# Root and reciprocal of the variance per output tile, and new ties for the first tiles' work

## The chip, the cores and the metric

The kernel runs on one core of a Trainium2 chip. That core has a matrix engine (PE; its weight loads are shown as PEld), a vector engine (DVE), an activation engine (ACT), GpSimd (POOL), and a queue engine (SP) that issues nearly all transfers between the device memory and the on-chip memory. Each engine works through its own list of instructions in order; an instruction that waits holds up all that stands behind it on its engine. The metric is the device time of one execution in microseconds (us), as the median of several runs; lower is better.

## The reference, cut to what matters

The kernel computes one layer of an encoder for two requests of 512 and 1024 tokens (1536 in all, 1024 features), with 16 learned tokens put in front. The change touches the normalisation of the convolution branch:

```
z   = rms_norm(h) @ w_in              # gates, values, q, k, v
y   = depthwise_conv(val * sigmoid(glu)) + conv_b
mu  = mean(y)                         # over 1024 channels, per token
var = mean((y - mu)**2)
c   = silu((y - mu) * rsqrt(var + 1e-5) * ln_g + ln_b) * silu(c_gate)
a   = neighbourhood_attention(q, k, v) * silu(a_gate)
out = h + rms_norm([c ; a] @ w_out)
```

## The kernel before, in words

Three stages follow each other on PE. First the input projections and the convolution (the convolution's taps run on DVE). Then the attention: 8 pairs of heads, each with 3 groups of tokens in 2 halves. For each block PE makes scores (`ss`, L578), DVE and ACT make the softmax (`pt`, L585 to L591), PE transposes (`tp`, L600), ACT copies the transposed block (`pT`, L602), and PE weighs the values with it (`po`, L616). Between these blocks PE's list is filled with projections of 24 matrix products (`mm`, L180): the keys and queries of the next pair, and gates of the attention branch, whose results ACT copies out (`ag`, L342). The last six of these projections, for gates 6 and 7 in three groups, stand behind the last weighted values (`a_gate(6, 7)`, L706).

The last stage is the output product (`py`, L794), in 12 tiles t of 128 tokens. A tile has two parts of 8 feature blocks: part 0 is the convolution branch, part 1 the attention branch. `mix(t, part)` loads one part (`mx`) and its gate (`gt`), normalises (part 0 alone: L767 subtracts the mean, L768 multiplies by the reciprocal root, L770 is the Silu of 8 blocks), multiplies with the Silu of the gate (L771, L772), and splits the product in a high and a low half (`mh` on ACT, L773; `ml` on DVE for the tiles 0 and 1, else on POOL, L774). The buffers of part 0, `mx`, `gt` and `mb`, are single, and all tiles share them. The output weights are loaded in 16 blocks and split the same way (`load_wo`, L731 to L750: ACT casts, DVE subtracts); blocks 0 to 5, 8, 9, 12 and 13 come through two buffers `wraw` that the gates' weights use too, so that a load waits until an earlier block's split is done. For the tiles 0 and 1 the products are made together: part 0 of tile 0, part 0 of tile 1, then the parts 1 (L810 to L814).

Mean and variance of each token come from `statistics()` (L648), which runs in small steps between the attention's blocks. It stores both in a table `std` in device memory (L666). At its end it loads all variances as 128x12 (`rv`, L674), takes the root on ACT (L678) and the reciprocal on DVE (L679), and stores them back over the variances (L680), four bytes at each place. `moments(t)` (L752) loads the two rows of tile t, spread over the partitions, into `mb`.

The order on each engine is not the order of the program text: a scheduler with a model of the times lays the instructions out, engine by engine. `tc.issue_after(x)` puts each instruction of its block that runs on the engine of `x` behind `x` in that engine's list; it adds no wait by itself. Before the change part 0 of tile 0 is tied behind the last copy of a transposed block (`last_pt`, an ACT instruction, L776), and part 0 of tile 1 behind the copy of the last gate (`last_copy`, ACT, L782).

Of the kernel before, what the change touches and what calls it, by code (L numbers as in the profile page):

```python
# [10 lines left out]
F32 = mybir.dt.float32  # L11
F32R = mybir.dt.float32r
AF = mybir.ActivationFunctionType
ALU = mybir.AluOpType
# [6 lines left out]
TG = TP + TS  # L21
# [72 lines left out]
def tile_encoder(ctx: ExitStack, tc: tile.TileContext, mt, xn, w_main, w_v, wo, cw, cb, lg, lb, pg, postg, rbt, rmask, y):  # L94
    nc = tc.nc
# [3 lines left out]
    mad = [tc.dram_tile((DC, 128, 512), F32, name=f"mad{g}") for g in range(3)]  # L99
# [3 lines left out]
    std = tc.dram_tile((2, TG), F32, name="std")  # L103

    const = ctx.enter_context(tc.tile_pool(name="const", bufs=1))
# [10 lines left out]
    nc.vector.memset(eps_sb[:, 1:2], 1e-5)  # L116

    ident = const.tile([128, 128], F32, name="ident")
    rv = const.tile([128, TG // 128], F32, name="rv")
    sel = const.tile([128, 16], F32, name="sel")  # L120
    cw_sb = const.tile([128, DC, 32], F32, name="cw_sb")
    cb_sb = const.tile([128, DC], F32, name="cb_sb")
# [158 lines left out]
        nc.scalar.copy(out=zc.rearrange("p (b r c) -> p b r c", r=8, c=8), in_=z[:, i].rearrange("p (r b c) -> p b r c", r=8, b=8))  # L281
        nc.sync.dma_start(zs[i][c], zc)

    vws, metas, last_copy = {}, [], [None]

    def load_v(qv):
        raws, his, los = [], [], []
# [46 lines left out]
    def gates(base, dst, cs):  # L334

        ws = [use_w(base + c) for c in cs]
        for g in range(3):
            for c, (wh, wl) in zip(cs, ws):
                ps = new_mm()
                proj(ps, wh, wl, 16 + g * 512, 16 + g * 512 + 512)  # L340
                gt = gpool.tile([128, 512], F32, name="ag", tag="ag", bufs=2)
                last_copy[0] = nc.scalar.copy(out=gt, in_=ps).ins  # L342
                nc.sync.dma_start(dst[g][c], gt)
                yield

# [219 lines left out]
    def scores(p, g, hf):  # L565
        if hf == 0:
            load_values(p, g)
        kh, kl = kbufs[p]
        qh, ql = qbuf.pop((p, g, hf))
        R8 = GR[g]["R"] * 8  # L570
        for jj in range(4):
            j = hf * 4 + jj
            b0, nk, key, _, _, e = block(g, j)
            ra, rn, ro = GR[g][key]
            w = rn * 8
            ss = ps_s.tile([128, 512], F32, name="ss")
            for i, (q, k) in enumerate(((qh, kh), (qh, kl), (ql, kh))):
                last_qk[0] = nc.tensor.matmul(ss[:, :nk * w], lhsT=q[:, jj].rearrange("p h x -> p (h x)"),  # L578
                                 rhs=k[:, b0:b0 + nk, ra:ra + rn, :].rearrange("p b r c -> p b (r c)"),
                                 start=(i == 0), stop=(i == 2))  # L580
            sv_ = ss[:, :nk * w].rearrange("p (k x) -> p k x", k=nk)[:, :, ro * 8:ro * 8 + R8]
            pt = apool.tile([128, 312], F32, name="pt", bufs=PTB)
            pv = pt[:, :nk * R8]
            sm = apool.tile([128, 4], F32, name="sm", bufs=8)
            nc.vector.tensor_tensor_reduce(out=pv.rearrange("p (k x) -> p k x", k=nk), in0=sv_,  # L585
                                           in1=e.rearrange("p k r c -> p k (r c)"), scale=1.0,
                                           scalar=-3.0e38, op0=ALU.add, op1=ALU.max, accum_out=sm[:, 0:1])
            nc.vector.tensor_scalar(out=sm[:, 1:2], in0=sm[:, 0:1], scalar1=-1.0, scalar2=None, op0=ALU.mult)  # L588
            last[0] = nc.scalar.activation(out=pv, in_=pv, func=AF.Exp, bias=sm[:, 1:2], scale=1.0, accum_out=sm[:, 2:3])  # L589
            nc.vector.reciprocal(sm[:, 3:4], sm[:, 2:3])  # L590
            nc.vector.tensor_scalar(out=pv, in0=pv, scalar1=sm[:, 3:4], scalar2=None, op0=ALU.mult)  # L591
            pts[p, g, j] = pv

    def transposes(p, g, hf):
# [10 lines left out]
    def weighted(p, g, hf):  # L605
        if hf == 0:
            pos[p, g] = ps_o.tile([128, 8, 64], F32, name="po")
        po, vt = pos[p, g], vts[p, g]
        for j in range(hf * 4, hf * 4 + 4):
            b0, _, _, nt, kt, _ = block(g, j)  # L610
            pT = pTs.pop((p, g, j))
            for k in range(nt):
                for h in range(2):
                    hs = slice(h * 64, h * 64 + 64)
                    v = vt[:, k, b0, hs] if g == 0 else vt[:kt, b0 + k, hs]
                    last_pv[0] = nc.tensor.matmul(po[hs, j, :], lhsT=v, rhs=pT[:kt, k * 128 + h * 64:k * 128 + h * 64 + 64],  # L616
                                                  start=(k == 0), stop=(k == nt - 1)).ins
        if hf == 1:
            mo = apool.tile([128, 512], F32, name="mo", bufs=1)
            nc.vector.tensor_copy(out=mo, in_=pos.pop((p, g)).rearrange("p j x -> p (j x)"))  # L620
            nc.sync.dma_start(mad[g][p], mo)

    def inner_gates():
        for p in (3, 4, 5):
# [23 lines left out]
    def statistics():  # L648
        for t in range(TG // 128):
            tsl = slice(t * 128, t * 128 + 128)  # L650
            hx = []
            for k in range(2):
                x = gpool.tile([128, 512], F32, name="ag", tag="ag", bufs=2).rearrange("p (c t) -> p c t", c=8)
                a = t % 4 * 128 + k * 64
                nc.sync.dma_start(x, zs[t // 4][:, :, a:a + 64].rearrange("c p t -> p c t"))
                hx.append((x, slice(k * 64, k * 64 + 64)))
            yield
            for moment in range(2):
                for x, sl in hx:
                    nc.vector.tensor_reduce(out=ms[:, sl], in_=x.rearrange("p c t -> p t c"), op=ALU.add, axis=mybir.AxisListType.X)  # L660
                yield
                ps = new_mm()
                with tc.issue_after(last_mm[0]):
                    nc.tensor.matmul(ps[:, :128], lhsT=ones, rhs=ms, start=True, stop=True)
                nc.scalar.copy(out=row[0:1], in_=ps[0:1, :128])
                nc.sync.dma_start(std[moment:moment + 1, tsl], row[0:1])  # L666
                if moment == 0:
                    for x, sl in hx:
                        nc.vector.tensor_tensor(out=x, in0=x, in1=ps[:, sl].unsqueeze(1).broadcast_to([128, 8, 64]), op=ALU.subtract)
                        nc.scalar.activation(out=x, in_=x, func=AF.Square)  # L670

        s = std[1:2]
        var = bass.AP(s.tensor, s.offset, [[1, 128], [128, TG // 128]])
        nc.sync.dma_start(rv, var)  # L674
        yield
        yield
        with tc.issue_after(last[0].ins):
            nc.scalar.activation(out=rv, in_=rv, func=AF.Sqrt, bias=eps_sb[:, 1:2])  # L678
        nc.vector.reciprocal(rv, rv)  # L679
        nc.sync.dma_start(var, rv)  # L680
        yield

    stats = statistics()
    knext, last_pv, last_pt = [None], [None], [None]
    e_build(0)
    groups = [(p, g, hf) for p in range(NPAIR) for g in range(3) for hf in range(2)]
    for n in range(len(groups) + 2):
# [64 lines left out]
    def moments(t):  # L752
        tsl = slice(t * 128, t * 128 + 128)
        s = std[:, tsl]
        nc.sync.dma_start(mb, bass.AP(s.tensor, s.offset, [[0, 128], [TG, 2], [1, 128]]))

    def mix(t, parts=(0, 1)):
        for part in parts:
            if part == 0:
                moments(t)  # L760
            mx, gt = mxs[part], gts[part]
            mh, ml = [x[t % 2 * 2 + part] for x in (mhs, mls)]
            g, csl = t // 4, slice(t % 4 * 128, t % 4 * 128 + 128)
            nc.sync.dma_start(mx, (zs, mad)[part][g][:, :, csl].rearrange("c p t -> p c t"))
            nc.sync.dma_start(gt, (cgd, agd)[part][g][:, :, csl].rearrange("c p t -> p c t"))
            if part == 0:
                nc.vector.tensor_tensor(out=mx, in0=mx, in1=mb[:, 0:1].broadcast_to([128, 8, 128]), op=ALU.subtract)  # L767
                nc.vector.tensor_tensor(out=mx, in0=mx, in1=mb[:, 1:2].broadcast_to([128, 8, 128]), op=ALU.mult)  # L768
                for c in range(8):
                    nc.scalar.activation(out=mx[:, c], in_=mx[:, c], func=AF.Silu, scale=lg_sb[:, c:c + 1], bias=lb_sb[:, c:c + 1])  # L770
            nc.scalar.activation(out=gt, in_=gt, func=AF.Silu)  # L771
            nc.vector.tensor_tensor(out=mx, in0=mx, in1=gt, op=ALU.mult)  # L772
            nc.scalar.copy(out=mh, in_=mx)  # L773
            (nc.vector if t < MLT else nc.gpsimd).tensor_tensor(out=ml, in0=mx, in1=mh.bitcast(F32), op=ALU.subtract)  # L774

    with tc.issue_after(last_pt[0]):  # L776
        mix(0, (0,))
    for n in range(16):
        if n == 6:
            mix(0, (1,))  # L780
        elif n == 8:
            with tc.issue_after(last_copy[0]):  # L782
                mix(1, (0,))
        elif n == 10:
            mix(1, (1,))
        load_wo(n)
    pgb = wop.tile([128, D], F32, name="pgb")
# [124 lines left out]
```

## Time and profile before

| what | value |
|---|---|
| median of 3 runs | 1469.12 us (1467.73 to 1469.58) |
| the profiled execution | 1470.34 us |
| its span in the trace | 1468.2 us |
| mean granted clock of PE | 0.993 |
| PE busy | 1437.6 us (98%) |
| DVE, ACT, POOL busy | 1012.4, 562.8, 254.9 us |

The trace shows one execution. A row of the chain of waits gives a piece of the work that ended last: its start, its length, and the engine and line, or the transfer. A row of a timeline gives start and length of an instruction, and in brackets how long its engine stood idle before it and for what. A row of windows gives the busy time of each engine in a stretch, with the number of instructions in brackets, the granted clock of PE (1.00 is its upper level, 0.50 half of it), the share of the transfer engines that was busy, and GB/s.

### The profile page before, as it was taken

Reading aid. Unit: us, or ns where it says so; the run is one execution under the profiler, and the core shown is the slowest. Engines: PE = TensorE matmul, PEld = TensorE weight load, DVE = VectorE, ACT = ScalarE, POOL = GpSimd, SP = SyncE. Lnnn points to the kernel's source line nnn. Section 1 sums busy time; section 2 is a strip of 40 time slices with the busy share of each in tenths; the row PEclk is TensorE's granted clock in tenths of the full one; section 3 lists DMA queues with packets and bytes.
Section 4 is the critical chain, followed back from the end, with each engine's and each line's share of the span. In section 5 each row is a group of like instructions: output and inputs, shape, how many; then the busy total and the mean of one; then the engine's idle time right before and its main releaser. Section 6 shows DMA issues by size and latency. Waiting matters only on the chain.

```text
span 1468.2 us, 24129 instructions
## 1 busy us (share of the span) xinstructions
PE 1437.6 (98%) x9536; PEld 1239.6 (84%) x9536; DVE 1012.4 (69%) x1739; ACT 562.8 (38%) x1299; POOL 254.9 (17%) x188
## 2 busy tenths in 40 slices
PE   7999999999999999999999999999979989999998
PEld 6988998988998888888888988888868878888886
DVE  6599999998999899846776777767544364342431
ACT  7311112112111111235564555655534466544440
POOL 2042022112101211221111211111101002122120
PEclk9999999999999999999999999999989999999999
DMA  8113113312231212242232232332322495544521
GB/s 266 42 48 117 47 55 110 93 40 93 76 92 50 96 51 86 105 105 75 77 88 79 84 82 77 88 87 83 86 62 87 159 294 145 151 147 136 164 89 43
DMA packets 153464, 145.19 MB, mean 99 GB/s; under 512 B 37216, under 2 KB 125432, under 8 KB 153352
## 3 DMA queue, kind: packets, MB, share of 16 engines
q1 hardware_dynamic: 153352, 143.67, 32.5%
q8 instruction: 74, 1.21, 0.3%
q14 instruction: 38, 0.31, 0.1%
HBM read 105.35 MB, written 42.72 MB: 101 GB/s over the span
## 4 chain that ended last, share of the span: by engine, by line
PE 90%; DMA 4%; ACT 2%; DVE 2%; POOL 1%; issue 1%; DVEq 0%; SPq 0%; ACTq 0%; POOLq 0%
PE mm L180 36%; PE py L794 18%; PE tp L180 9%; PE mm L322 5%; PE ss L578 5%; PE po L180 5%; PE po L616 4%; PE tp L600 4%; PE tp L322 3%; DMA wraw<-in_wo 1%; PE po L322 1%; POOL vl L142 1%; DMA std<-rv 1%; DMA yo<-in_wo 0%; ACT mx L770 0%
## 5 line engine op out<-in xcount | busy, mean ns | idle before, releaser
L180 PE MATMUL mm<-uw,whi 128*128 128x512 f32 (+2 forms) x1904 | 562.1, 372 | 0.0
L272 DVE SCALAR_TENSOR_TENSOR z<-ub,cw_sb,z 128x1536 f32<-128x1536 f32 (+2 forms) x270 | 498.7, 1854 | 8.1
L180 PEld LDWEIGHTS mm<-uw,whi 128*128 128x128 f32 x1904 | 342.5, 188 | 55.4 <-issue 1.3
L180 PE MATMUL mm<-uw,wlo 128*128 128x512 f32 (+2 forms) x952 | 352.6, 371 | 1.1 <-POOL wlo L142 1.1
L142 POOL TENSOR_TENSOR wlo<-wraw,whi 128x1024 fp32r<-128x1024 f32 x48 | 129.0, 2689 | 542.2 <-ACT whi L141 537.5
L180 PEld LDWEIGHTS mm<-uw,wlo 128*128 128x128 f32 x952 | 179.4, 188 | 27.2 <-POOL wlo L142 1.4
L794 PE MATMUL py<-uw,mh 128*128 128x512 f32 x576 | 182.0, 397 | 0.0
L180 PE MATMUL tp<-uw,whi 128*128 128x512 f32 (+2 forms) x512 | 132.9, 344 | 0.0
L589 ACT ACTIVATE pt<-pt,sm 128x216 f32<-128x216 f32 (+4 forms) x192 | 97.2, 507 | 92.9 <-DVE sm L588 79.9
L794 PEld LDWEIGHTS py<-uw,mh 128*128 128x128 f32 x576 | 108.7, 189 | 25.9
L794 PE MATMUL py<-uw,ml 128*128 128x512 f32 x288 | 113.8, 395 | 0.0
L602 ACT COPY pT<-tp 108x256 f32<-108x256 f32 (+4 forms) x192 | 77.9, 419 | 81.9 <-PE tp L600 57.1
L180 PEld LDWEIGHTS tp<-uw,whi 128*128 128x128 f32 x512 | 89.3, 188 | 11.6
L767 DVE TENSOR_TENSOR mx<-mx,mb 128x1024 f32<-128x1024 f32 x12 | 14.7, 1225 | 121.2 <-DMA mx<-zs 110.0
L585 DVE CUSTOM_DVE_ANT_0 pt<-ss,ei 128x216 f32<-128x216 f32 (+2 forms) x144 | 62.6, 437 | 50.2 <-PE ss L578 26.6
L180 PE MATMUL tp<-uw,wlo 128*128 128x512 f32 (+2 forms) x256 | 88.1, 344 | 0.0
L600 PE MATMUL tp<-ident,pt 128*96 128x128 f32 (+2 forms) x480 | 85.5, 275 | 0.3 <-ACT pT L602 0.2
L774 POOL TENSOR_TENSOR ml<-mx,mh 128x1024 fp32r<-128x1024 f32 x20 | 48.2, 2430 | 211.5 <-ACT mh L773 193.7
L322 PE MATMUL mm<-vh,uw 128*128 128x256 f32 x448 | 83.5, 285 | 0.7 <-DVE uw L208 0.5
L591 DVE TENSOR_SCALAR pt<-pt,sm 128x216 f32<-128x216 f32 (+4 forms) x192 | 70.7, 368 | 4.9
L578 PE MATMUL ss<-kh,qh 128*128 128x264 f32 (+3 forms) x192 | 65.3, 340 | 9.0 <-DVE sm L585 9.0
L141 ACT CAST whi<-wraw 128x1024 fp32r<-128x1024 f32 x48 | 50.2, 1047 | 61.6 <-DMA wraw<-in_w_main 19.1
(170 smaller groups left out, 2183.1 us busy)
## 6 DMA issues: line engine op xcount, KB each, us to landing
wraw<-in_w_main SPq DMA_DIRECT2D x48, 512.0 KB
xt<-in_xn SPq DMA_DIRECT2D x12, 512.0 KB
vd<-vs SPq DMA_DIRECT2D x96, 64.0 KB
zs<-zc SPq DMA_DIRECT2D x24, 256.0 KB
cgd<-ag SPq DMA_DIRECT2D x24, 256.0 KB
agd<-ag SPq DMA_DIRECT2D x24, 256.0 KB
ag<-zs SPq DMA_DIRECT2D x24, 256.0 KB
mad<-mo SPq DMA_DIRECT2D x24, 256.0 KB
```

The source lines that it names most:

```text
L142: eng.tensor_tensor(out=lo, in0=raw, in1=hi.bitcast(F32), op=ALU.subtract)
L180: last_mm[0] = nc.tensor.matmul(ps[:, :n], lhsT=w[:, dc, :], rhs=u[dc // 4][:, dc % 4, :], start=(dc == 0 and i == 0), stop=(dc == DC - 1 ...
L272: nc.vector.scalar_tensor_tensor(out=zv, in0=ub[:, a:b, k:k + 512], scalar=cw_sb[:, c, k:k + 1], in1=zv, op0=ALU.mult, op1=ALU.add)
L322: nc.tensor.matmul(ps[:, :256], lhsT=u[dc // 4][:, dc % 4, :], rhs=w[dc // 4][:, dc % 4, :], start=(dc == 0 and i == 0), stop=(dc == DC - ...
L578: last_qk[0] = nc.tensor.matmul(ss[:, :nk * w], lhsT=q[:, jj].rearrange("p h x -> p (h x)"), rhs=k[:, b0:b0 + nk, ra:ra + rn, :].rearrange ...
L585: nc.vector.tensor_tensor_reduce(out=pv.rearrange("p (k x) -> p k x", k=nk), in0=sv_, in1=e.rearrange("p k r c -> p k (r c)"), scale=1.0, ...
L589: last[0] = nc.scalar.activation(out=pv, in_=pv, func=AF.Exp, bias=sm[:, 1:2], scale=1.0, accum_out=sm[:, 2:3])
L591: nc.vector.tensor_scalar(out=pv, in0=pv, scalar1=sm[:, 3:4], scalar2=None, op0=ALU.mult)
L600: nc.tensor.transpose(out=tp[:kt, k * 128:k * 128 + 128], in_=pv[:, k * kt:k * kt + kt], identity=ident)
L602: last_pt[0] = nc.scalar.copy(out=pT[:kt, :nt * 128], in_=tp[:kt, :nt * 128]).ins
L616: last_pv[0] = nc.tensor.matmul(po[hs, j, :], lhsT=v, rhs=pT[:kt, k * 128 + h * 64:k * 128 + h * 64 + 64], start=(k == 0), stop=(k == nt - ...
L794: nc.tensor.matmul(pss[hf], lhsT=m[e // 8][:, e % 8], rhs=w[e][:, hf * 512:hf * 512 + 512], start=(n == 0 and i == 0), stop=(n == 15 and i ...
```

## The change

The last step of `statistics()` goes: the load of the variances, the root, the reciprocal and the store. `moments(t)` takes the root (ACT) and the reciprocal (DVE) of the variance itself, on the 128x128 half of `mb`, once for each of the 12 tiles. Part 0 of tile 0 is tied behind three instructions now: the last `pT` copy (ACT), the last multiplication of a softmax (`last_norm`, DVE) and the store of the last group but one of the attention's results (`stores[-2]`, SP). Part 0 of tile 1 is tied behind the copy of the fourth of the last six gates (`copies[-3]`) in place of the last. In the loop that loads the output weights, tile 1's part 0 is written at n = 6, tile 0's part 1 at 10 and tile 1's part 1 at 12 (before: tile 0's part 1 at 6, tile 1's parts at 8 and 10).

```diff
@@ statistics()
-        s = std[1:2]
-        var = bass.AP(s.tensor, s.offset, [[1, 128], [128, TG // 128]])
-        nc.sync.dma_start(rv, var)
-        yield
-        yield
-        with tc.issue_after(last[0].ins):
-            nc.scalar.activation(out=rv, in_=rv, func=AF.Sqrt, bias=eps_sb[:, 1:2])
-        nc.vector.reciprocal(rv, rv)
-        nc.sync.dma_start(var, rv)
-        yield
...
@@ moments(t)
         nc.sync.dma_start(mb, bass.AP(s.tensor, s.offset, [[0, 128], [TG, 2], [1, 128]]))
+        nc.scalar.activation(out=mb[:, 1], in_=mb[:, 1], func=AF.Sqrt, bias=eps_sb[:, 1:2])
+        nc.vector.reciprocal(mb[:, 1], mb[:, 1])
...
-    with tc.issue_after(last_pt[0]):
+    with tc.issue_after(last_pt[0]), tc.issue_after(last_norm[0]), tc.issue_after(stores[-2]):
         mix(0, (0,))
     for n in range(16):
         if n == 6:
-            mix(0, (1,))
-        elif n == 8:
-            with tc.issue_after(last_copy[0]):
+            with tc.issue_after(copies[-3]):
                 mix(1, (0,))
         elif n == 10:
+            mix(0, (1,))
+        elif n == 12:
             mix(1, (1,))
         load_wo(n)
```

The lines of the changed kernel lie up to 11 lower in number: L767, L768 and L591 of before are L757, L758 and L590 there; the new root and reciprocal are L744 and L745.

On DVE, at the start of the last pair's work, tile 0's first two operations (`mx` with `mb`) stood between the softmax operations of the attention before:

```order
L588 TENSOR_SCALAR sm_11033<-sm_11033 128x1
L590 RECIPROCAL sm_11033<-sm_11033 128x1
L767 TENSOR_TENSOR mx_12146<-mx_12146,mb_12149 128x1024
L591 TENSOR_SCALAR pt_11032<-pt_11032,sm_11033 128x216
L585 ISA pt_11043,sm_11044<-ss_11039,ei0_5362 128x216
L585 ISA sm_11044 128x1
L768 TENSOR_TENSOR mx_12146<-mx_12146,mb_12149 128x1024
```

In the changed kernel the same operations on DVE stand behind the attention's last softmax:

```order
L587 TENSOR_SCALAR sm_11708<-sm_11708 128x1
L589 RECIPROCAL sm_11708<-sm_11708 128x1
L590 TENSOR_SCALAR pt_11707<-pt_11707,sm_11708 128x208
L619 COPY mo_11736<-po_11562 128x512
L757 TENSOR_TENSOR mx_12141<-mx_12141,mb_12144 128x1024
L745 RECIPROCAL mb_12144<-mb_12144 128x128
L619 COPY mo_11948<-po_11824 128x512
L758 TENSOR_TENSOR mx_12141<-mx_12141,mb_12144 128x1024
```

No softmax operation is queued behind them any more; what is left behind them is the copy of the attention's last result (`mo`).

On ACT, at the end of the attention (`pT_11901` is the last transposed block, `ag_11928` the last gate but six, `whi_11958` the cast of the last gate's weights), before:

```order
L602 COPY pT_11901<-tp_11898 104x256
L770 ACT_TABLE_LOAD
L770 ACTIVATE mx_12146<-mx_12146,lb_sb_98,lg_sb_97 128x128 x8
L771 ACTIVATE gt_12147<-gt_12147 128x1024
L342 COPY ag_11928<-mm_11903 128x512
L141 CAST whi_11958<-wraw_11956 128x1024
L748 CAST woh0_12184<-wraw_12182 128x1024
L773 CAST mh_12148<-mx_12146 128x1024
```

And after (`pT_11896` is the last block, `ag_11923` and `whi_11953` the same gate and weights):

```order
L341 COPY ag_11923<-mm_11898 128x512
L140 CAST whi_11953<-wraw_11951 128x1024
L601 COPY pT_11896<-tp_11893 104x256
L744 ACT_TABLE_LOAD
L744 ACTIVATE mb_12144<-mb_12144,eps_sb_89 128x128
L761 ACT_TABLE_LOAD
L761 ACTIVATE gt_12142<-gt_12142 128x1024
L760 ACTIVATE mx_12141<-mx_12141,lb_sb_97,lg_sb_96 128x128 x8
L736 CAST woh0_12181<-wraw_12179 128x1024
L736 CAST woh1_12187<-wraw_12185 128x1024
L341 COPY ag_11982<-mm_11957 128x512
L763 CAST mh_12143<-mx_12141 128x1024
```

The gate's copy and the cast of the last gate's weights have moved ahead of the last `pT`, and a root with two table loads stands behind it.

On ACT, ahead of the high half of tile 1's part 0 (`mh1`), before; `ag_12127` is the last gate's copy:

```order
L342 COPY ag_12127<-mm_12102 128x512
L770 ACTIVATE mx_12146<-mx_12146,lb_sb_98,lg_sb_97 128x128 x8
L771 ACTIVATE gt_12147<-gt_12147 128x1024
L748 CAST uw_12275<-wraw_12273 128x1024
L773 CAST mh2_12160<-mx2_12153 128x1024
L748 CAST uw_12280<-wraw_12278 128x1024
L773 CAST mh1_12159<-mx_12146 128x1024
```

After; `ag_12122` is the last gate's copy, `ag_12094` the fifth of the last six:

```order
L760 ACTIVATE mx_12141<-mx_12141,lb_sb_97,lg_sb_96 128x128 x8
L761 ACTIVATE gt2_12149<-gt2_12149 128x1024
L341 COPY ag_12094<-mm_12069 128x512
L744 ACT_TABLE_LOAD
L744 ACTIVATE mb_12144<-mb_12144,eps_sb_89 128x128
L736 CAST uw_12247<-wraw_12245 128x1024
L736 CAST uw_12258<-xr_12256 128x1024
L341 COPY ag_12122<-mm_12097 128x512
L736 CAST uw_12263<-yo_12261 128x1024
L763 CAST mh1_12154<-mx_12141 128x1024
```

Tile 1's Silu has moved ahead of the last two gates' copies, and its `mh1` now needs the output weights up to block 11 instead of 13, but a third root (tile 2's) stands ahead of it.

## Rows read from the trace of the kernel before

**Rows 1.** Waits of PE: engine, line, waited for; us in total, times, longest.
```profile
PE ss L578 <- DVE sm L585: 9.0, 2, 8.7
PE py L794 <- ACT mh L773: 3.9, 1, 3.9
```

**Rows 2.** Chain of waits from 1062 to 1078 us: start, length, what.
```profile
1062.39 10.93 DMA std<-rv
1073.34 4.05 DMA mb<-std
1077.42 1.22 DVE mx L767
```

**Rows 3.** Windows over both waits: busy us (instructions), PE clock, transfer share, GB/s.
```profile
1070.50:1079.24 8.74, 0.00 (x1) 0.00 (x0) 1.82 (x5) 0.00 (x0) 0.00 (x0) 0.64 0.29 45
1079.24:1083.10 3.86, 3.86 (x12) 3.15 (x13) 2.94 (x9) 2.02 (x6) 0.00 (x0) 0.50 0.13 35
1186.76:1199.45 12.69, 12.69 (x55) 9.95 (x53) 7.83 (x7) 10.04 (x17) 0.00 (x0) 1.00 0.97 331
1199.45:1203.37 3.92, 0.00 (x0) 0.00 (x1) 3.79 (x4) 3.92 (x6) 0.00 (x0) 0.90 1.02 326
1203.37:1209.40 6.03, 6.03 (x14) 4.77 (x15) 5.47 (x5) 3.75 (x4) 0.00 (x0) 0.50 1.02 274
```

**Rows 4.** Timeline of ACT, the end of the attention to tile 1's part 0.
```profile
1151.04 0.75 ACT L602 COPY pT<-tp 104x384 f32<-104x384 f32 x2 [4.19 <-PE tp L600]
1151.80 1.28 ACT L770 ACT_TABLE_LOAD   x1
1153.10 3.19 ACT L770 ACTIVATE mx<-mx,lb_sb,lg_sb 128x128 f32<-128x128 f32 x8
1156.20 1.04 ACT L771 ACTIVATE gt<-gt 128x1024 f32<-128x1024 f32 x1
1157.15 0.56 ACT L342 COPY ag<-mm 128x512 f32<-128x512 f32 x1
1157.61 1.05 ACT L141 CAST whi<-wraw 128x1024 fp32r<-128x1024 f32 x1
...
1202.27 1.05 ACT L773 CAST mh<-mx 128x1024 fp32r<-128x1024 f32 x1
```

**Rows 5.** Timeline of PE: the last weighted values of the attention.
```profile
1152.25 1.50 PE L616 MATMUL po<-pT,vt 104*64 104x64 f32 x44
```

**Rows 6.** Windows of line L180 alone: the last six gates.
```profile
1153.68:1186.76 33.08, 33.08 (x144) 26.96 (x144) 1.00 0.80 257
```

**Rows 7.** Waits of ACT from 1176 to 1203 us.
```profile
ACT uw L748 <- DMA wraw<-in_wo: 3.3, 3, 2.1
ACT gt L771 <- DMA gt<-agd: 2.1, 1, 2.1
ACT uw L748 <- DMA xr<-in_wo: 1.8, 1, 1.8
```

**Rows 8.** Timeline of SP: issue of the second last store, and of weight block 1.
```profile
1139.41 0.32 SPq L621 DMA_DIRECT2D mad<-mo  x1
...
1162.27 0.33 SPq L738 DMA_DIRECT2D wraw<-in_wo  x1
```

**Rows 9.** Groups of DVE's reciprocals: count, busy us, mean ns, idle before.
```profile
L590 DVE RECIPROCAL sm<-sm 128x1 f32<-128x1 f32 x192 | 31.1, 162 | 55.4 <-ACT pt L589 52.7
L679 DVE RECIPROCAL rv<-rv 128x12 f32<-128x12 f32 x1 | 0.2, 228 | 1.0 <-ACT rv L678 1.0
```

**Rows 10.** Window over the steady tiles: busy us (instructions) of PE, PEld, DVE, ACT, POOL.
```profile
1300.00:1440.00 140.00, 140.00 (x603) 112.82 (x602) 42.43 (x56) 61.16 (x104) 28.93 (x12) 1.00 0.41 122
```

**Rows 11.** Timeline: a steady tile's halves on ACT and POOL, its first product.
```profile
1328.40 1.98 ACT L773 CAST mh<-mx 128x1024 fp32r<-128x1024 f32 x2
...
1329.51 4.81 POOL L774 TENSOR_TENSOR ml<-mx,mh 128x1024 fp32r<-128x1024 f32 x2 [18.62 <-ACT mh L773]
...
1350.17 0.40 PE L794 MATMUL py<-woh,mh 128*128 128x512 f32 x1
```

More of the change, by code (lines that the diff above doesn't have):

```diff
@@ L118, in tile_encoder @@
     ident = const.tile([128, 128], F32, name="ident")
-    rv = const.tile([128, TG // 128], F32, name="rv")
     sel = const.tile([128, 16], F32, name="sel")
@@ L282, in store_z @@
         nc.sync.dma_start(zs[i][c], zc)
-    vws, metas, last_copy = {}, [], [None]
+    vws, metas, copies = {}, [], []
     def load_v(qv):
@@ L341, in gates @@
                 gt = gpool.tile([128, 512], F32, name="ag", tag="ag", bufs=2)
-                last_copy[0] = nc.scalar.copy(out=gt, in_=ps).ins
+                copies.append(nc.scalar.copy(out=gt, in_=ps).ins)
                 nc.sync.dma_start(dst[g][c], gt)
@@ L590, in scores @@
             nc.vector.reciprocal(sm[:, 3:4], sm[:, 2:3])
-            nc.vector.tensor_scalar(out=pv, in0=pv, scalar1=sm[:, 3:4], scalar2=None, op0=ALU.mult)
+            last_norm[0] = nc.vector.tensor_scalar(out=pv, in0=pv, scalar1=sm[:, 3:4], scalar2=None, op0=ALU.mult).ins
             pts[p, g, j] = pv
@@ L620, in weighted @@
             nc.vector.tensor_copy(out=mo, in_=pos.pop((p, g)).rearrange("p j x -> p (j x)"))
-            nc.sync.dma_start(mad[g][p], mo)
+            stores.append(nc.sync.dma_start(mad[g][p], mo).ins)
     def inner_gates():
@@ L670, in statistics @@
                         nc.scalar.activation(out=x, in_=x, func=AF.Square)
-        s = std[1:2]
-        var = bass.AP(s.tensor, s.offset, [[1, 128], [128, TG // 128]])
-        nc.sync.dma_start(rv, var)
-        yield
-        yield
-        with tc.issue_after(last[0].ins):
-            nc.scalar.activation(out=rv, in_=rv, func=AF.Sqrt, bias=eps_sb[:, 1:2])
-        nc.vector.reciprocal(rv, rv)
-        nc.sync.dma_start(var, rv)
-        yield
     stats = statistics()
-    knext, last_pv, last_pt = [None], [None], [None]
+    knext, last_pv, last_pt, last_norm, stores = [None], [None], [None], [None], []
     e_build(0)
```

## The prediction

> **What bounds the kernel now.** I read the engines' busy shares first: PE is busy for 1437.6 of 1468.2 us, and no other engine comes near. So the time is PE's work plus what PE waits, and the list of its waits comes next. Outside the first 20 us it has two that count: 8.7 us for DVE's score operation L585, and 3.9 us for a high half `mh` from ACT [rows 1].
>
> The chain of waits shows what stood behind the first [rows 2]. The stored-back reciprocals took 10.93 us to land, since they go out four bytes at a time; the load of `mb` behind them took 4.05 us; and only then could DVE run L767, which had stood at the head of its list since before. The order of DVE shows softmax operations queued behind L767, and PE needs their buffers. So a tile's preparation, not due for another 100 us, stopped the attention.
>
> The windows show what each wait cost beside itself [rows 3]. PE came back from the first at half clock (0.50) for 3.86 us, so 1.93 us of work's worth was lost; after the second for 6.03 us, so 3.02 us. The clock had fallen while PE stood idle, and it rose again with PE busy. First wait: 8.74 + 1.93 = 10.67 us. Second: 3.92 + 3.02 = 6.94 us. Together 17.6 us, the most that this change can plainly give back.
>
> **The change part by part.** The profiled execution took 1470.34 us, 1.22 over the median of the runs; I make the sum on it and take 1.22 off at the end.
>
> *The first wait goes.* There is no store of reciprocals left for `mb` to wait for, and L767 and L768 now stand behind the last softmax on DVE. Behind them waits only the copy of the attention's last result, for which no PE instruction waits soon. Tile 0's loads are tied behind the store issued at 1139.41 in the trace, 12.4 us before the last `pT` copy ends at 1151.79 [rows 4, 8]; the measured 4.05 us for `mb` fits into that three times, though the two loads of 512 KB beside it have no row of their own here. Gain 10.67 us. The removed root, its two table loads and the 12-column reciprocal ran beside busy PE work; I count them as nothing.
>
> *A new small wait at the end of the attention.* The order of ACT now has the copy of a gate and the cast of the last gate's weights between the third last and the last `pT`. On PE the weighted values of the last block stand right behind 18 of the 22 in their group: 18/22 of 1.50 us is 1.2 us, and with two transposes some 1.4 us after the gate's products end [rows 5]. ACT needs from there about 0.4 us to notice, 0.46 for the copy, 0.95 for the cast and 0.4 for `pT`: 2.2 to 2.5 us (starts in rows 4; notice and `pT` are estimates from neighbouring starts). PE waits about 1.0 us. Bounds: nothing, if the cast ran earlier, and 2 us. I take 1.0.
>
> *The second wait.* Count from P, the end of the last `pT`. Before, tile 1's `mh` was done at 1203.32, P + 51.5, because the weight blocks came late: block 1 was issued at P + 10.5, as its buffer was held by the last gate's weights until their cast and split [rows 4, 8]. Every later block waits for a cast and a subtraction of an earlier one. In the new order the last gate's cast stands ahead of P, so the buffer is free about 2.4 us after it; the load then stands on SP behind the store of the last result, which needs root, reciprocal and copy: 1.28 + 0.40 + 0.92 + 0.7, so about P + 3.5. The chain of blocks starts some 7 us earlier.
>
> The floor is then ACT's own work after the fourth gate. In the new order that is three gate copies, three table loads, two roots, two gate Silus, the eight Silus, seven weight casts and two casts of `mh`. At the spacings of rows 4 (0.46, 1.28, 0.40, 0.95, 3.10, 0.95, and 1.05 for the last): 1.4 + 3.8 + 0.8 + 1.9 + 3.1 + 6.7 + 2.0 = 19.7 us. PE has in that time two gates (a third of 33.08, 11.0 us) and 48 products of tile 0, at 12.69/54 each 11.3 us: 22.3 us [rows 3, 6]. With about half a us until ACT starts the copy, ACT has 2 us in hand, and loses them where it waits for loads. Before, those waits in this stretch came to 7.2 us [rows 7]. With the chain 7 us earlier most should be gone; I take 3 us left, so PE waits 1.0 us, too short, I think, for the clock to fall: it was still at its upper level in most of the 3.92 us before 1203.37 (0.90 on average) [rows 3]. Bounds: nothing, and the full 7.2 us less 2.
>
> *The root and reciprocal in every tile.* The root is 0.40 us, taken as one of the 128x128 Silus (3.19/8) [rows 4]; below it lies the 0.3 us of a one-column root, and it needs two table loads more, 2.56 us. The reciprocal of 128 columns: 0.162 us for one column and 0.228 for 12 [rows 9] give 0.006 us a column, so 0.92 us; bounds 0.23 (as 12 columns) and 2.4 (as 12 columns times 10.7). In tiles 2 to 11 that is 3.0 us of ACT and 0.9 of DVE a tile. PE takes 96 products a tile, 22.3 us; ACT is busy for 44% of that and DVE for 30% [rows 10]. The halves of a tile are ready far ahead: `ml` at 1334.3 for a tile whose first product is at 1350.17, 15.9 us [rows 11]. So nothing, on PE's path. If that cover went, 3.0 us times 10 tiles would be 30 us.
>
> A rule speaks against this. A table load here took 1.28 us, and the next operation started 0.02 us after it [rows 4]. The Trainium skill (ScalarE: Activation LUTs, What ACT_TABLE_LOAD costs) states 1283 ns for the load and a drain of about 1380 ns beside it, 2.66 us a switch, and its rules for authors say to do all of one set before switching. By that, an estimate, three switches after the fourth gate would cost ACT 4.1 us more and PE 4.1 us less what is in hand. The trace agrees with the load and shows no drain.
>
> Sum: 1470.34 - 10.67 - 6.94 + 1.0 + 1.0 = 1454.7, less 1.22 is **1453.5 us**.
>
> **The rivals.**
>
> 1. *The second wait stays.* ACT's 7.2 us of waits for loads stay, since transfers were saturated in that stretch (shares 0.97 and 1.02) [rows 3], and tile 0's two loads have moved nearer to it. PE waits 5.2 us, and then loses 3 to the clock: 1453.5 - 1.0 + 8.2 = 1460.7. For it: the saturation. Against it: the same bytes, started earlier.
> 2. *Table switches cost more than the load*, as much again each time. Three in the critical stretch make PE wait 2 to 3 us more, with the clock's fall up to 6: about 1458. Against it: the 0.02 us above.
> 3. *The new lay-out of the last pair has more small waits* like the one found. PE's order differs from before over the last 100 us of the attention. Five or six such waits: about 1459. Against it: before, the same scheduler left none above 0.3 us there but the large one.
> 4. *The queue is blocked at its head*, the case that ends slower. On SP, tile 1's `mb` waits for tile 0's L768, and the loads of weight blocks 2 to 15 stand behind it. L768 needs tile 0's `mx`, `mb`, root and reciprocal, which now all come in the last stage. If `mx` came over 14 us after its issue, each further us would delay every weight block. PE has 16.6 us of gain to lose here; with 3 of the clock and the 2 in hand that is a delay of 15.6 us, so a load of some 30 us. At 33 us: about 1473. Against it: the longest landing on the chain here was 10.93 us, for four-byte pieces.
>
> **How the numbers follow.** Forecast 0.58; rival 1 0.19; rival 2 0.05; rival 3 0.10; rival 4 0.08, half of it just short of the break-even and half past it. A difference of 0.2% (2.9 us) is about the least that runs of this kernel can tell from none: faster 0.92, same 0.04, slower 0.04. The likeliest case alone spans 1451.5 (both small waits nothing) to 1456.5 (2 and 3 us). The range adds the 1 us by which runs of before differ below, and goes to rival 1 above, which covers rivals 2 and 3: 1450.5 to 1461.
>
> **What would show it.** Right: no wait of PE for L585 above 1 us, no root of 128x12, granted clock 1.00 from 1000 us to the tail; a PE wait of about 1 us just before the last weighted values; `mh` of tile 1 within 2 us of PE's need; tile spacing still 22.3 us, with two further table loads and a root of 0.4 us in each. Wrong: a stretch at half clock near 1190 us (rival 1), a gap of over 1 us behind each table load (2), several waits for `pT` or `pt` between 1060 and 1140 (3), SP standing long at `mb` and weight blocks landing late (4).

## The result, and the profile after

The changed kernel takes 1460.11 us (median of 4 runs, 1459.00 to 1460.43) against 1469.06 for the kernel before beside it: a ratio of 0.9939, interval 0.9922 to 0.9956. It is faster by 9 us, where I had forecast 15.6; the range held the time, but it stands on its first rival (the second wait stays, 1460.7), not on the likeliest case of 1453.5. The profiled execution took 1460.28 us. Two of the executions timed for the experiments ran at a mean granted clock of 0.70 and 0.75 (1889.83 and 1772.54 us), and the times and ratios here leave them out.

PE's waits from 1040 to 1260 us in the changed kernel (the view of [rows 1]):

```profile
PE py L784 <- ACT mh L763: 3.8, 1, 3.8
PE py L784 <- DVE ml L764: 1.8, 1, 1.8
PE po L615 <- ACT pT L601: 0.5, 1, 0.5
```

The large wait for the softmax is gone. The new small one before the last weighted values is there, with 0.5 us. The wait for tile 1's high half `mh` is as long as before, and one for its low half `ml` follows it. The three instructions on PE's timeline, with the idle time ahead of each in brackets:

```profile
1141.37 0.45 PE L615 MATMUL po<-pT,vt 104*64 104x64 f32 x8 [0.48 <-ACT pT L601]
...
1189.88 0.50 PE L784 MATMUL py<-woh,mh 128*128 128x512 f32 x1 [3.82 <-ACT mh L763]
1192.58 0.80 PE L784 MATMUL py<-woh,ml 128*128 128x512 f32 x1 [1.84 <-DVE ml L764]
```

The windows from there on (columns as in [rows 3]) show the clock at half:

```profile
1189.88:1192.58 2.70, 0.86 (x3) 0.30 (x3) 2.70 (x4) 2.68 (x3) 0.00 (x0) 0.58 0.95 304
1192.58:1197.50 4.92, 4.92 (x12) 3.95 (x13) 3.71 (x4) 4.70 (x6) 0.00 (x0) 0.54 1.05 383
1300.00:1440.00 140.00, 140.00 (x603) 112.70 (x602) 46.86 (x65) 72.86 (x117) 29.06 (x12) 1.00 0.42 124
```

So the second wait costs 3.82 + 1.84 of idle time, and of the clock 0.46 x 4.92 + 0.42 x 0.86 = 2.6: 8.3 us, against 6.94 before. The third row is the steady tiles: ACT has risen from 61.16 to 72.86 us and DVE from 42.43 to 46.86 [rows 10], and PE still works the whole 140 us.

Why the half came late is on ACT's timeline, from the copy of the second of the last six gates to the root of tile 1, and further on the root of tile 2 and tile 1's high half:

```profile
1153.44 0.59 ACT L341 COPY ag<-mm 128x512 f32<-128x512 f32 x1 [1.21 <-PE mm L179]
1159.06 1.05 ACT L736 CAST uw<-wraw 128x1024 fp32r<-128x1024 f32 x1 [5.04 <-DMA wraw<-in_wo]
1160.41 1.05 ACT L736 CAST uw<-wraw 128x1024 fp32r<-128x1024 f32 x1 [0.29 <-DMA wraw<-in_wo]
1161.36 0.58 ACT L341 COPY ag<-mm 128x512 f32<-128x512 f32 x1
1165.45 1.05 ACT L736 CAST uw<-wraw 128x1024 fp32r<-128x1024 f32 x1 [3.51 <-DMA wraw<-in_wo]
1168.99 1.06 ACT L761 ACTIVATE gt<-gt 128x1024 f32<-128x1024 f32 x1 [2.49 <-DMA gt<-agd]
1169.95 0.57 ACT L341 COPY ag<-mm 128x512 f32<-128x512 f32 x1
1170.54 1.28 ACT L744 ACT_TABLE_LOAD   x1
1171.84 0.40 ACT L744 ACTIVATE mb<-mb,eps_sb 128x128 f32<-128x128 f32 x1
...
1183.87 1.28 ACT L744 ACT_TABLE_LOAD   x1
1185.17 0.40 ACT L744 ACTIVATE mb<-mb,eps_sb 128x128 f32<-128x128 f32 x1
...
1188.78 1.04 ACT L763 CAST mh<-mx 128x1024 fp32r<-128x1024 f32 x1
```

The copy at 1169.95 is the fourth gate's. PE had that gate's products done at about 1163.9 (the last six gates start at 1141.8, and four of six are two thirds of 33.08 us [rows 6]). The copy came 6.0 us later, because ACT's list has ahead of it a cast that waited 3.51 us for its weights, to 1165.45, and tile 0's gate Silu that then waited 2.49 us for its load. The chain of waits tells what that load waited for:

```profile
1154.08 8.56 DMA agd<-ag
1162.69 6.27 DMA gt<-agd
```

It is the second gate's own store and the load back. All of tile 1's work was tied behind the fourth gate's copy, so ACT could begin none of it in the 11.3 us that it stood idle between 1154 and 1169. From the copy's start to the end of `mh` there were then 19.87 us without one wait.

DVE tells why the low half came later still:

```profile
1186.76 1.23 DVE L762 TENSOR_TENSOR mx<-mx,gt 128x1024 f32<-128x1024 f32 x1 [0.20 <-DMA mx<-mad]
1187.90 1.22 DVE L737 TENSOR_TENSOR uw<-wraw,uw 128x1024 fp32r<-128x1024 f32 x1
1189.04 1.22 DVE L737 TENSOR_TENSOR uw<-xr,uw 128x1024 fp32r<-128x1024 f32 x1
1190.17 1.22 DVE L737 TENSOR_TENSOR uw<-yo,uw 128x1024 fp32r<-128x1024 f32 x1
1191.31 1.22 DVE L764 TENSOR_TENSOR ml<-mx,mh 128x1024 fp32r<-128x1024 f32 x1
```

L762 works on tile 1's attention half, loaded from `mad`; three subtractions of weight blocks and then the low half stand behind it. The chain of waits has what that load waited for:

```profile
1178.99 1.23 DVE ml L764
...
1180.24 6.50 DMA mx<-mad
```

The low half of tile 0's attention half had to leave the buffer first, and the load itself then took 6.50 us. On SP's queue it also stands behind the weight blocks 9, 10 and 11, issued from 1176.83 to 1179.10, whose buffers come free behind casts on ACT. The cast ahead of that low half (1177.35) and those of the weights (from 1174.51) all stand behind the late copy. So both halves hang on it.

### The profile page after: what moved, and what is told of

It reads as the page before. It is cut to its first block, busy times and chain, and to the rows that moved or that the text cites. A ratio compares the mean times of both kernels' runs of the same rounds, so it can differ in the third digit from the quotient of the medians.

```text
span 1458.1 us, 24177 instructions
## 1 busy us (share of the span) xinstructions
PE 1433.9 (98%) x9536; PEld 1236.5 (85%) x9536; DVE 1021.3 (70%) x1750; ACT 594.7 (41%) x1331; POOL 253.4 (17%) x188
## 4 chain that ended last, share of the span: by engine, by line
PE 91%; DMA 3%; DVE 2%; ACT 1%; POOL 1%; issue 1%; SPq 0%; DVEq 0%; ACTq 0%; POOLq 0%
PE mm L179 37%; PE py L784 18%; PE tp L179 9%; PE mm L321 5%; PE ss L577 5%; PE po L179 5%; PE po L615 4%; PE tp L599 4%; PE tp L321 3%; PE po L321 1%; POOL vl L141 1%; DMA xt<-in_xn 1%; DMA agd<-ag 1%; DMA mx<-mad 0%; DMA gt<-agd 0%
## 5 line engine op out<-in xcount | busy, mean ns | idle before, releaser
L757 DVE TENSOR_TENSOR mx<-mx,mb 128x1024 f32<-128x1024 f32 x12 | 14.7, 1224 | 105.6 <-DMA mx<-zs 105.6
L764 POOL TENSOR_TENSOR ml<-mx,mh 128x1024 fp32r<-128x1024 f32 x20 | 48.5, 2443 | 219.0 <-ACT mh L763 207.2
L590 DVE TENSOR_SCALAR pt<-pt,sm 128x216 f32<-128x216 f32 (+4 forms) x192 | 71.6, 373 | 4.9
L179 PE MATMUL po<-uw,whi 128*128 128x512 f32 (+2 forms) x272 | 72.9, 347 | 0.0
```

The costliest lines, as they stand in the source:

```text
L179: last_mm[0] = nc.tensor.matmul(ps[:, :n], lhsT=w[:, dc, :], rhs=u[dc // 4][:, dc % 4, :], start=(dc == 0 and i == 0), stop=(dc == DC - 1 ...
L590: last_norm[0] = nc.vector.tensor_scalar(out=pv, in0=pv, scalar1=sm[:, 3:4], scalar2=None, op0=ALU.mult).ins
```

## The experiments

All are timed over five rounds beside the kernel before, which took 1468.36 us (the first three and the third gate) and 1468.66 us (the others) there, against 1469.06 us beside the changed kernel. Differences between two versions are of their medians and can be off by some 0.7 us for that.

**The root alone.** The kernel before, with this part of the change only:

```diff
-        [rv: load, root, reciprocal and store back, in statistics()]
         nc.sync.dma_start(mb, ...)
+        nc.scalar.activation(out=mb[:, 1], in_=mb[:, 1], func=AF.Sqrt, bias=eps_sb[:, 1:2])
+        nc.vector.reciprocal(mb[:, 1], mb[:, 1])
```

> The kernel before with one part of the change: root and reciprocal in each tile, no ties, the old order of the loop. Theory A (each wait has its own cause: the first is DVE's list head standing for the stored reciprocals, the second is ACT's own work between the fourth gate's copy and tile 1's high half): the store is gone, so the first wait falls from 8.7 us to 0 to 2; tile 1's root and two table loads stay behind the last gate's copy, where by the order 15.4 us of ACT's work now lie up to the high half against 8.4 in the trace of before, so the second wait grows by 3 to 7 us from 3.9. Sum 1469.1 - 10.7 + 3 to 7: 1462 to 1466. Theory B (the second wait is late weight loads, DMA being full, and the root costs ACT nothing there): second wait as before, 1458.5.

Measured: 1459.13 us, ratio 0.9936 (0.9922 to 0.9950), as much as the whole change. DVE still has the subtraction (L758) between softmax operations, and it stands there for 3.04 us; PE does not feel it:

```profile
1062.55 1.22 DVE L758 TENSOR_TENSOR mx<-mx,mb 128x1024 f32<-128x1024 f32 x1 [3.04 <-DMA mx<-zs]
```

PE's one large wait, on its timeline, is that for `mh`:

```profile
1196.82 0.79 PE L785 MATMUL py<-woh,mh 128*128 128x512 f32 x1 [5.07 <-ACT mh L764]
```

PE's window behind it (PE's busy time alone, then clock, transfer share, GB/s) has the clock at half:

```profile
1196.82:1199.95 3.13, 3.13 (x7) 0.50 0.87 244
```

That is 5.07 + 1.57 = 6.6 us. The first wait was as theory A had it. Its 1462 to 1466 was too high: it took the need for the high half as fixed, but PE's list had changed with ACT's: between the last gate and the wait it now had 73 products where the changed kernel has 48, so about half of tile 0's attention half stood ahead of tile 1, and the need came at 1191.75, 5.7 us later than in the changed kernel. The time fits theory B as well; the next run parts them.

**The ties and the order alone.** The changed kernel, with the stored reciprocals of before:

```diff
-        nc.scalar.activation(out=mb[:, 1], in_=mb[:, 1], func=AF.Sqrt, bias=eps_sb[:, 1:2])
-        nc.vector.reciprocal(mb[:, 1], mb[:, 1])
+        [rv: load, root, reciprocal and store back, in statistics()]
```

> The changed kernel without the per-tile root: statistics store the reciprocals as before, but all ties and the order of the loop are those of the change. Theory A: the first wait is gone (the subtraction stands behind the last softmax on DVE), and ACT has 12.6 us of work from the fourth gate's copy to tile 1's high half instead of 19.7; even with that copy 6 us late, this is under PE's 22.3 us, so the second wait is gone too: 1460.1 - 8.2 = 1452, and PE waits under 1 us for the high half. Theory B (late loads decide): the second wait stays at 4 to 6 us, 1459 to 1460.

Measured: 1453.09 us, ratio 0.9894 (0.9880 to 0.9908). The list of PE's waits from 1020 to 1260 us has one entry:

```profile
PE po L616 <- ACT pT L602: 0.5, 1, 0.5
```

On ACT's timeline, the fourth gate's copy and tile 1's high half:

```profile
1168.44 0.57 ACT L342 COPY ag<-mm 128x512 f32<-128x512 f32 x1
...
1180.06 1.04 ACT L773 CAST mh<-mx 128x1024 fp32r<-128x1024 f32 x1
```

Theory B has fallen: ACT waited 8.3 us for the same loads ahead of that copy, the copy came nearly as late as in the changed kernel, and there is no second wait. ACT took 12.66 us from the copy to the end of the high half, not 19.87; what the root adds there is what makes PE wait. So each part removes the first wait by itself (which of the ties does it was not run apart), and the root, put in with the ties, costs 7.0 us (1460.11 - 1453.09).

**The gate Silu behind the fourth gate's copy.** This takes away the cause of the late copy in the changed kernel.

```diff
         elif n == 10:
-            mix(0, (1,))
+            with tc.issue_after(copies[-3]):
+                mix(0, (1,))
```

> The changed kernel with one more tie: the gate Silu of tile 0's attention half stands behind the fourth gate's copy on ACT, not ahead of it. Theory A: the copy no longer waits for that gate's store and load, starts at 1166.5 instead of 1169.95 (behind the cast that waits for its weights), and tile 1's high half is done at 1187.4 instead of 1189.8; PE waits about 3.3 us for both halves instead of 5.7: 1456 to 1457.5. Theory B (weight loads decide): high half as late as now, 1460.

Measured: 1454.18 us, ratio 0.9900 (0.9886 to 0.9915). The copy on ACT's timeline:

```profile
1165.93 0.58 ACT L341 COPY ag<-mm 128x512 f32<-128x512 f32 x1
```

The two waits on PE's:

```profile
1187.29 0.50 PE L785 MATMUL py<-woh,mh 128*128 128x512 f32 x1 [1.59 <-ACT mh L763]
1188.55 0.50 PE L785 MATMUL py<-woh,ml 128*128 128x512 f32 x1 [0.52 <-DVE ml L764]
```

And PE's window behind them:

```profile
1189.07:1195.00 5.93, 5.93 (x27) 1.00 1.08 339
```

The copy comes 4.0 us sooner and the high half at 1187.2, as expected. The time is 2 us better than expected, since the low half followed sooner and the clock did not fall: 3.5 us of idle time and 2.6 of clock went with this one tie. The copy's place is not all of it: the scheduler laid out DVE's list anew, and the multiplication of tile 1's attention half (L762), ahead of the low half in the changed kernel, starts behind it here, at 1188.41.

**The table loads.** The changed kernel with the same order on ACT, without three table loads:

```diff
-        ... func=AF.Sqrt, bias=eps_sb[:, 1:2])
+        ... func=AF.Square if t in (1, 2) else AF.Sqrt, bias=eps_sb[:, 1:2])
```

> The changed kernel with the root of tiles 1 and 2 replaced by a square (this part of the result is left out), an operation of the same 128x128 form that needs no other table. The order on ACT stays, less three table loads of 1.28 us between the fourth gate's copy and tile 1's high half. Theory A (ACT's own work after the copy): 19.9 us become 16.0, so the high half ends at 1185.9, just when PE wants it; the low half comes some 2 us behind. Of 8.2 us 2 to 3 stay: 1454 to 1455. If each load also had a drain of 1.4 us that the rows hide, 4 us more go and nothing is left: 1452. Theory C (the copy's late start is all that counts, and ACT's work behind it is covered): 1459 to 1460.

Measured: 1455.50 us, ratio 0.9910 (0.9897 to 0.9924), 0.5 us above what was expected. On ACT's timeline the fourth gate's copy and the high half:

```profile
1168.80 0.57 ACT L341 COPY ag<-mm 128x512 f32<-128x512 f32 x1
...
1183.37 1.05 ACT L763 CAST mh<-mx 128x1024 fp32r<-128x1024 f32 x1
```

On PE's the only wait left for a half:

```profile
1188.63 0.51 PE L784 MATMUL py<-woh,ml 128*128 128x512 f32 x1 [2.11 <-DVE ml L764]
```

From the copy's start to the end of the high half it is 15.62 us, against 19.87: three loads are worth 4.25 us, 1.42 each, where one takes 1.28 in the rows. By the Trainium skill (ScalarE: Activation LUTs, What ACT_TABLE_LOAD costs), a switch costs 1283 ns and a drain of some 1380 ns beside it; by that, an estimate, three would be 8.0 us. This run agrees with the load and leaves at most 0.14 us a switch for a drain. The rows account for that too: a load, and the operation behind it, start some 0.02 us after the end of what stands ahead, where two operations without a load between them overlap by some 0.10 us (the version called Both, below, has both cases). Theory C has fallen, too: with the copy only 1.15 us sooner, shorter work behind it gives 4.6 us back.

**Tile 2's root behind tile 1's high half.**

```diff
-        if t > 1:
+        if t == 2:
+            with tc.issue_after(casts[1, 0]):
+                mix(t)
+        elif t > 2:
             mix(t)
```

(`casts[1, 0]` is the copy to tile 1's first high half.)

> The changed kernel with one more tie: tile 2's root, which ACT now does ahead of tile 1's high half since its moments are there, stands behind that half. A table load and a root (1.28 + 0.40) leave the stretch. Theory A: the high half ends 1.7 us sooner, at 1188.1, PE waits 4.0 instead of 5.7 us in two pieces, and the clock may fall for less time: 1457.5 to 1458.5. Theory C: 1460.

Measured: 1459.27 us, ratio 0.9932 (0.9919 to 0.9946): 0.8 us where 1.6 to 2.6 were expected, and on the medians alone not to be told from none. PE's timeline:

```profile
1188.23 0.50 PE L786 MATMUL py<-woh,mh 128*128 128x512 f32 x1 [2.38 <-ACT mh L765]
1192.61 0.80 PE L786 MATMUL py<-woh,ml 128*128 128x512 f32 x1 [3.64 <-DVE ml L766]
```

The high half came 1.7 us sooner, as expected, and the low half at the same time as in the changed kernel. L764, the multiply that was L762, started on DVE no sooner:

```profile
1186.79 1.23 DVE L764 TENSOR_TENSOR mx<-mx,gt 128x1024 f32<-128x1024 f32 x1 [3.04 <-DMA mx<-mad]
```

Its load hangs on casts that lie ahead of the removed root. I had taken the low half as following the high one; it has a chain of its own.

**Tile 1's work behind the third gate.**

```diff
-            with tc.issue_after(copies[-3]):
+            with tc.issue_after(copies[-4]):
                 mix(1, (0,))
```

> The changed kernel with tile 1's first work on ACT (root, table loads, gate Silu, eight Silus) tied behind the third gate of the last six instead of the fourth. ACT then does it where it now stands idle for weights and a gate (3.5 and 2.5 us), and from the fourth gate's copy to tile 1's high half only 6.9 us of work are left by the order. Theory A: the high half is done near 1179, 7 us ahead of PE's need, the second wait and its half clock are gone: 1452, the best so far. Theory B (loads decide): the high half is not the last to come; PE waits for a weight block instead, 1457 to 1460.

Measured: 1451.21 us (1451.56 with all four executions), ratio 0.9882 (0.9866 to 0.9897). No rows of this version are read; those of the next stand in for them.

**Both.** The third gate, and tile 2's root behind the high half.

> The version with tile 1's work behind the third gate, and tile 2's root tied behind tile 1's high half. By the order 6.2 us of ACT's work lie between the fourth gate's copy and the high half. Theory A: the first version (1451.6) had no second wait left, so nothing more is to be had: 1451 to 1452; the profile shows no wait of PE for either half, a wait of 0.5 us for the last pT, and a granted clock of 1.00 from 1000 us to the tail. If 1 us or more is gained, the first version still lost time there.

Measured: 1450.97 us, ratio 0.9880 (0.9867 to 0.9894), the fastest, and not to be told from the version before it. On ACT, where the changed kernel waited 3.51 and 2.49 us, there is now tile 1's work:

```profile
1160.78 0.58 ACT L341 COPY ag<-mm 128x512 f32<-128x512 f32 x1
1161.37 1.28 ACT L744 ACT_TABLE_LOAD   x1
1162.66 0.40 ACT L744 ACTIVATE mb<-mb,eps_sb 128x128 f32<-128x128 f32 x1
1163.09 1.28 ACT L763 ACT_TABLE_LOAD   x1
1164.38 1.06 ACT L763 ACTIVATE gt<-gt 128x1024 f32<-128x1024 f32 x1
1165.35 1.03 ACT L736 CAST uw<-wraw 128x1024 fp32r<-128x1024 f32 x1
1166.29 3.18 ACT L762 ACTIVATE mx<-mx,lb_sb,lg_sb 128x128 f32<-128x128 f32 x8
1169.38 1.05 ACT L763 ACTIVATE gt<-gt 128x1024 f32<-128x1024 f32 x1
1170.33 0.56 ACT L341 COPY ag<-mm 128x512 f32<-128x512 f32 x1
```

The fourth gate's copy is no earlier than in the changed kernel. Yet PE waits for neither half: what lay behind that copy now lies ahead of it, in idle time.

**The per-tile work twice.** The version with the third gate, and in tiles 3 to 11:

```diff
+            nc.scalar.activation(out=row, in_=mb[:, 1], func=AF.Sqrt, bias=eps_sb[:, 1:2])
+            extra = nc.scalar.activation(out=row, in_=row, func=AF.Silu).ins
+            nc.vector.reciprocal(row, row)
+            with tc.issue_after(extra):
                 nc.scalar.activation(out=mb[:, 1], in_=mb[:, 1], func=AF.Sqrt, bias=eps_sb[:, 1:2])
```

> The version with tile 1's work behind the third gate, and in tiles 3 to 11 a second root, a Silu of 128x128 behind it and a second reciprocal, all into a scratch tile (they change no result): per tile two table loads, two operations and a reciprocal more, some 3.4 us of ACT and 0.95 of DVE. My step that the per-tile work is hidden: ACT then works 15 of 22.3 us a tile, no wait of PE, the same time within 1 us: 1451 to 1452.5. If it lay on the path: 9 x 3.4 = 31 us more, 1482; if only each tile's first products felt it, 1453 to 1460.

Measured: 1451.36 us, ratio 0.9882 (0.9869 to 0.9896), against 1451.21 without. The steady tiles:

```profile
1300.00:1440.00 140.00, 140.00 (x603) 112.72 (x602) 52.86 (x70) 84.92 (x135) 28.94 (x12) 1.00 0.41 124
```

ACT works 84.92 of 140 us, 12 more than in the changed kernel, and PE has not lost a tenth of one.

## Why the prediction was right and wrong, step by step

(a) *The first wait goes*: right, in place and size. The root alone and the ties alone each show it, where I had argued only for the two together. What cost PE time was the store of single elements with `mb` behind it; a subtraction that stood 3.04 us among the softmax operations cost PE nothing.

(b) *A new small wait*: right, 0.48 us where I took 1.0.

(c) *The second wait nearly goes*: wrong, and this is the step that failed. The start of the weight blocks was right: block 1's load went out 3.7 us after the last `pT`, where I had 3.5. The floor was right too: ACT's work after the copy I put at 19.7 us, and it took 19.87. What failed is "about half a us until ACT starts the copy": it took 6.0. I had looked for ACT's waits for loads behind the copy and left 3 us of them there; there were none, since all 11.3 us lay ahead of it. With that one term put right the prediction's own sum gives a wait of 19.87 + 6.0 - 22.3 = 3.6 us; it was 3.82, and the low half's 1.84 came on top. I never asked what stands ahead of the copy on ACT, and what the load of the gate Silu there waits for. Rival 1 had the time right and half of the reason: ACT's waits for loads did stay, 11.3 us where it had 7.2, but they lay ahead of the copy. Such waits do not decide alone: with the ties alone ACT had 8.3 us of them there, and PE waited for neither half. What decides is that the copy comes late by its place in ACT's list (the Silu moved: 5.9 us) together with the work tied behind it (no table loads: 4.6; no per-tile root: 7.0; tile 1's work ahead of it: 8.9). I had not seen the low half's own chain at all. That the time fell into the range is rival 1's place in it, and not a merit of the likeliest case.

(d) *The root and reciprocal of each tile are hidden*: right from tile 3 on, as the doubled work shows, with durations as estimated: root 0.40, reciprocal 0.95 where I took 0.92. Tile 1's are not hidden: they are in step (c). So are tile 2's by their place in the list, though moving them alone gave no more than 0.8 us.

(e) *The drain*: not seen, in the rows or by the run without three loads. Rival 2 has fallen. Rivals 3 and 4 did not show: there is one small wait at the attention's end, and no wait of PE for a weight block.

The sum: 1470.34 - 10.67 + 0.48 + (8.3 - 6.94) = 1461.5; the profiled execution took 1460.28. Of what is left, the stretch ahead of all that the change touches accounts for more than all: the last store of the moments is issued 1.62 us sooner in the changed kernel's execution (SP's timeline, first the kernel before, then the changed one).

```profile
1029.76 0.24 SPq L666 DMA_DIRECT2D std<-cw_sb  x1
```
```profile
1028.14 0.25 SPq L665 DMA_DIRECT2D std<-cw_sb  x1
```

With that the sum is 1459.9, 0.4 us below the time. Not all of the 1.62 us is chance. PE's last product of L302 (L301 in the changed kernel) starts at 221.2 us before and 220.6 after, and at 220.4 to 221.4 in the other versions: that differs from execution to execution. But from there to the first score of the attention PE takes 425.9 us before and 426.0 with the ties alone, which keep the stored reciprocals, and 424.9 to 425.0 us in the changed kernel and the six other versions read here, which have none, with the same number of weight loads on the way. So 1 us came with the program that has no stored reciprocals, in a stage where I had counted nothing; why, no run here shows.

## What to carry to other kernels

Where work is tied behind an instruction, work out when that instruction can start, from everything that stands ahead of it on its engine and from what each of those waits for; the length of the work behind it is only half of the sum. A tie is best put just ahead of idle time: the same work of tile 1 came with 8.3 us of waiting and half clock behind the fourth gate's copy and with none behind the third's. And when a part of a change is priced at nothing because other work covers it, price it apart in the first rounds of the loop, where that cover isn't there yet.

## What the runs showed of the hardware that was not expected

After PE's waits of 1.59 and 0.52 us, and of 2.11 us, the granted clock stayed at 1.00; after waits of 3.64 us and of 5.07 us it was at 0.50, its lower level of 1.2 GHz, for some 4 and 3 us. In the version with tile 2's root behind the high half, the clock fell in the second of two waits and stayed at half for 4.3 us (windows of PE):

```profile
1188.23:1192.61 4.38, 0.74 (x3) 0.71 0.83 260
1192.61:1196.90 4.29, 4.29 (x10) 0.50 1.03 396
```

So a wait made shorter can give back more than itself: from the changed kernel to the one with the Silu moved, 3.5 us less of waiting came with 2.6 us less lost to the clock.
